# One transpose for both heads' 64 extra keys in the two middle neighbourhood pairs of a one-core encoder kernel

## The chip, the core and the metric

The kernel runs on one core of one Trainium2 chip. The core has five engines that work side by side and wait for one another by semaphores: TensorE (PE in the profile; its weight loads are listed as PEld), VectorE (DVE), ScalarE (ACT), GpSimd (POOL) and SyncE (SP, which here issues most of the DMAs). The metric is the device time of one execution in microseconds (us); lower is better.

## The reference

The network has two layers of width 1024 on 512 tokens. In each layer the normalised input is projected, three branches (differential attention, a convolution module, 2-D neighbourhood attention) work on parts of the projection and are merged by gates; a SwiGLU feed-forward network and a gated embedding follow. The change lies in the neighbourhood attention alone:

```
def neighbourhood_attention(qc, kc, vc, rpb):      # 8 heads of 64, grid of 8 rows x 64 columns
    ...
    s = jnp.einsum('bhwd,bhrwcd->bhwrc', q_r, kn).astype(jnp.float32) * scale
    ...
    a = jax.nn.softmax(s.reshape(B, HC, GRID_W, KR * NA_KC), axis=-1)
    ...
    return jnp.einsum('bhwrc,bhrwcd->bhwd', a, vn)
```

Every query sees all 8 rows and a window of 16 columns. The kernel orders the tokens column by column, so a tile of 128 queries (16 columns) needs a run of 256 neighbouring keys.

## The kernel before

**Precision.** Matrix products are made from fp32 numbers cut in two: a high half, which ScalarE writes by a copy into the type fp32r, and a low half, which VectorE writes by a subtraction (`split`, L156 to L158; its ScalarE part is recorded at L143, its VectorE part at L157). A projection takes three products per block (L177 to L179): high by high, high by low, low by high.

**The order of the work.** TensorE's order is the order in which the Python code emits it. The order on the other engines is made by a scheduler that takes, among the instructions that are ready in its own model of time, the one with the best priority; priority is the order of emission, unless `high_priority(offset=n)` moves an instruction n places forward. Weight blocks (`weights`) are fetched and split with such an offset of up to 400. The 31 taps of the convolution (L160 on VectorE, tile `conv_z`) are emitted a few at a time behind other VectorE work (`background`).

Attention is not written as one stage. It is cut into generators (`natten_unit`, `diff_unit`), whose steps are let in between the chunks of the projections: `tick` counts chunks, `later` queues units with a gap, and each `yield` says how many ticks pass before the unit's next step. So TensorE works on projections while the softmax of a unit runs elsewhere.

**A neighbourhood unit.** The 8 heads form 4 pairs (`pr` 0 to 3), the 512 queries 2 halves. One unit is one head (`u` 0 or 1) of a pair for one half: 16 units for a layer, 32 in all, in the order pair, half, head. In each unit there are two query tiles, and one of the two, the wide one, reaches 64 keys beyond the half's own 256 keys. A unit does this:

- scores of both tiles (L847), a minimum on VectorE (L725), exponentials on ScalarE, and then a ScalarE copy of each tile that scales it by the reciprocal sum (all ScalarE work is recorded at L143; tile `natten_e`);
- three ticks later the transposes of the probabilities: four of 128x128 into the PSUM tile `pt` for the half's own keys (L751), and a fifth into `pt2` for the extra keys (L753 in half 0, L749 in half 1). The fifth transposes 128 keys, of which the unit uses 64;
- the splits of `pt` (into tile `natten_pt`) and of the used half of `pt2` (into tile `natten_a`, named `p2` in the code). `p2` holds the high halves of the 64 keys on one half of the partitions and the low halves on the other;
- two ticks later the products with the values: four of 256 columns (L773) and one of 128 columns for the extra keys (L774; "edge product" below), into the PSUM tile `av`. One `av` of one bank serves both heads of a pair and half, and there is a single buffer of it;
- from `av` the output: a ScalarE copy of 64x256 (high half), a VectorE subtraction (low half) and a VectorE addition, all into tile `natten_y`.

`branch_c` consumes `natten_y` after all pairs, far later. PSUM tiles `pt` and `pt2` share the tag `tr` with two buffers. In pair 0 of layer 0 the splits have a priority of their own (`first`).

Of the kernel before, what the change touches and what calls it, by code (L numbers as in the profile page):

```python
# [20 lines left out]
P = 128  # L21
# [13 lines left out]
NW = 256  # L35
# [26 lines left out]
class Net:  # L62
# [228 lines left out]
    def build(self):  # L291
        nc, tc, a = self.nc, self.tc, self.a
        self.bufs = dict(wr=3, wh=3, wl=3, h=8, qk=2, kh=1, v=4, pt=2, y=5, z=5, x=4, t=7, rp=2,
                         e=2, a=3, r=3, ss=1, sm=8, rc=4, b=2, s=8)
        self.bg, self.w_ahead = BG, 400
        self.pbufs = dict(mm=3, sc=2, tr=2, av=1)
        with tc.tile_pool(name="sb", bufs=1) as self.pool, \
                tc.tile_pool(name="ps", bufs=1, space=PSUM) as self.psum, \
                tc.tile_pool(name="dr", bufs=1, space=DRAM) as dram:
            xs = dram.tile([KD, P, 512], F32, name="xs")  # L300
            self.pis = dram.tile([KD, P, 512], F32, name="pis")
            with tc.manual_schedule(engines={mybir.EngineType.PE}):
                h = self.opening()
                xsrc = a["xT"]
                for i in range(L):
                    h = self.layer(i, h, xsrc, xs)
                    xsrc = xs
# [80 lines left out]
    def small(self):  # L388

        for tag in ("ident", "ones"):  # L390
            self.sb(tag, [P, P], bufs=1)
        for tag in ("onesr", "zeror"):
            self.sb(tag, [P, P], F32R, bufs=1)
        for tag, n in (("b", 2 * NW), ("s", 10), ("sm", 8), ("rc", 4)):
# [9 lines left out]

    def consts(self):
        nc, a = self.nc, self.a
        self.zero_r = self.sb("zeror", [P, P], F32R, bufs=1)
        nc.vector.memset(self.zero_r.bitcast(F32), 0.0)
# [300 lines left out]
    def natten_unit(self, pr, half, u, st4, k2, st, box, y):  # L709

        nc, i = self.nc, self.i
        mm = nc.tensor.matmul
        head = 2 * pr + u
        b = self.sb("b", [P, 2, NW])
        with self.tc.high_priority(offset=100):
            nc.sync.dma_start(b, self.a["bias"][i, head, half])
        es = []
        m = self.sb("s", [P, 6])
        two = self.sb("e", [P, 2, NW + 64])
        for t in range(2):  # L720
# [15 lines left out]
            es.append((e, e[:, own]))  # L736
# [7 lines left out]
        for t, (e, _) in enumerate(es):  # L744
            qt = 2 * half + t
            c0 = 64 * (qt == 2)
            ts = slice(t * P, (t + 1) * P)
            if qt == 2:
                nc.tensor.transpose(pt2, e[:, 0:P], self.ident)  # L749
            for c in range(2):  # L750
                nc.tensor.transpose(pt[:, c, ts], e[:, c0 + c * P:c0 + (c + 1) * P], self.ident)  # L751
            if qt == 1:
                nc.tensor.transpose(pt2, e[:, NW - 64:NW + 64], self.ident)  # L753
            if half != t:
                ws = ts
        pp = self.sb("pt", [P, 2, 2, 256], F32R)
        er, eo = (slice(0, 64), slice(64, P))[::1 if half else -1]
# [10 lines left out]
        av = box[half][:, u]  # L768
        hc = u * 256 + (pr % 2) * P
        cols = slice(hc, hc + P)  # L770
        for n in range(2):
            for k in range(2):
                mm(av, vs[2 * half + n][:, g, cols], pp[:, k, n], start=n == k == 0, stop=False)  # L773
        mm(av[:, ws], vds[g][half][:, cols], p2, start=False, stop=True)  # L774


        qs = slice(half * 256, half * 256 + 256)
        rs, ro = (slice(0, 64), slice(64, P))[::-1 if u else 1]
# [814 lines left out]
```

## Time and profile before

| what | value |
|---|---|
| time, median of 3 runs | 1772.08 us (1771.78 to 1774.45) |
| the profiled execution's own time | 1772.31 us |
| its span, first to last instruction | 1770.5 us |
| TensorE matmul busy | 1764.0 us, 100% of the span |
| TensorE weight loads busy | 1550.4 us, 88% |
| VectorE busy | 1371.0 us, 77% |
| ScalarE busy | 898.3 us, 51% |
| GpSimd busy | 63.5 us, 4% |
| transposes of the neighbourhood units | 160 (128 at L751, 16 at L753, 16 at L749) |
| edge products | 32 (L774) |

The duration of a matmul in the records runs from its start to its modelled end, and matmuls overlap: a 512-column one is listed with about 390 ns, but the next starts about 227 ns after it. What an instruction costs TensorE is read from the distance of starts, not from the duration. The middle pairs' units lie at about 99 to 168 us (layer 0) and 977 to 1047 us (layer 1) of the span.

### The profile page before, as it was taken

To read this page: it belongs to the slowest core of one execution; us is meant where nothing else is said; L and a number is where in the kernel's file an instruction comes from. 1 tells how busy PE (TensorE), PEld (TensorE's weight loads), DVE (VectorE), ACT (ScalarE), POOL (GpSimd) and SP (SyncE) were. 2 spreads that over 40 slices of the span, in tenths; PEclk is the share of its full clock that TensorE was granted. 3 is DMA by queue.
4 is the path that set the end of the run, shared out by engine and by line. 5 is a ranking of instruction groups with operands and counts; after the bars stand their busy time and mean duration, and the time that the engine had idled before them with its cause. 6 is when DMAs were issued, how large, how long until landed. Compare 5 with 4: busy or idle time off the path is not lost.

```text
span 1770.5 us, 26539 instructions
## 1 busy us (share of the span) xinstructions
PE 1764.0 (100%) x10017; PEld 1550.4 (88%) x10017; DVE 1371.0 (77%) x2111; ACT 898.3 (51%) x1482; POOL 63.5 (4%) x102
## 2 busy tenths in 40 slices
PE   9999999999999999999999999999999999999998
PEld 7888888888899899898888888888888998998987
DVE  7689887997877577577796788869878775775776
ACT  5566556325665255255545665563356652542544
POOL 0000000000010000000000000000000100100000
PEclk9999999999999999999999999999999999999999
DMA  5666453335656366253537574423364762763432
GB/s 194 191 191 180 126 140 84 102 99 174 196 156 178 127 167 179 85 143 118 160 122 191 177 183 122 135 84 107 105 197 139 191 191 85 187 173 111 122 111 96
DMA packets 98672, 257.51 MB, mean 145 GB/s; under 512 B 12912, under 2 KB 18160, under 8 KB 98544
## 3 DMA queue, kind: packets, MB, share of 16 engines
q1 hardware_dynamic: 91200, 231.26, 42.0%
q0 software_dynamic: 6336, 23.07, 7.4%
q8 instruction: 79, 1.29, 0.3%
q10 hardware_dynamic: 1008, 1.48, 0.2%
q14 instruction: 49, 0.40, 0.1%
HBM read 216.44 MB, written 7.86 MB: 127 GB/s over the span
## 4 chain that ended last, share of the span: by engine, by line
PE 98%; DMA 1%; DVE 0%; ACT 0%; issue 0%; ACTq 0%
PE ffn_sc L1141 14%; PE ffn_av L1141 7%; PE ffn_mm L178 4%; PE ffn_mm L179 4%; PE ffn_mm L177 4%; PE ffn_tr L1141 4%; PE mergea_mm L179 2%; PE mergea_mm L177 2%; PE mergea_mm L178 2%; PE natten_mm L177 2%; PE diff_sc L847 2%; PE gatec_mm L178 2%; PE natten_mm L178 2%; PE diff_mm L177 2%; PE diff_mm L178 2%; PE natten_mm L179 2%
## 5 line engine op out<-in xcount | busy, mean ns | idle before, releaser
L143 ACT ACTIVATE ffn_wh<-ffn_wr 128x1024 fp32r<-128x1024 f32 (+1 forms) x114 | 116.6, 1028 | 193.3 <-PE ffn_mm L178 102.0
L160 DVE SCALAR_TENSOR_TENSOR conv_z<-glu_z,pre_par,conv_z 128x512 f32<-128x512 f32 x240 | 179.2, 747 | 3.0
L157 DVE TENSOR_TENSOR ffn_wl<-ffn_wr,ffn_wh 128x1024 fp32r<-128x1024 f32 (+1 forms) x114 | 135.1, 1185 | 53.3 <-ACT ffn_wh L143 52.8
L1141 PE MATMUL ffn_sc<-wo_h,ffn_wh 128*128 128x256 f32 x704 | 130.4, 283 | 0.0
L1141 PEld LDWEIGHTS ffn_sc<-wo_h,ffn_wh 128*128 128x128 f32 x704 | 110.4, 192 | 0.8
L1141 PE MATMUL ffn_sc<-wo_h,ffn_wl 128*128 128x256 f32 x352 | 99.6, 283 | 0.0
L177 PE MATMUL ffn_mm<-ffn_z,ffn_wh 128*128 128x512 f32 x240 | 93.4, 389 | 0.0
L178 PE MATMUL ffn_mm<-ffn_z,ffn_wh 128*128 128x512 f32 x240 | 93.4, 389 | 0.0
L179 PE MATMUL ffn_mm<-ffn_z,ffn_wl 128*128 128x512 f32 x240 | 93.4, 389 | 0.0
L157 DVE TENSOR_TENSOR ffn_t<-ffn_mm,wo_r 128x512 f32<-128x512 f32 x48 | 33.1, 690 | 69.2 <-PE ffn_mm L179 69.2
L157 DVE TENSOR_TENSOR ffn_wl<-ffn_rp,ffn_wh 128x1024 fp32r<-128x1024 f32 x44 | 53.8, 1223 | 30.1 <-ACT ffn_wh L143 30.1
L143 ACT ACTIVATE mergea_wh<-mergea_wr 128x1024 fp32r<-128x1024 f32 (+1 forms) x32 | 27.1, 847 | 88.8 <-PE mergea_mm L178 80.4
L1141 PEld LDWEIGHTS ffn_sc<-wo_h,ffn_wl 128*128 128x128 f32 x352 | 67.5, 192 | 0.0
L1141 PE MATMUL ffn_sc<-wo_qk,ffn_wh 128*128 128x256 f32 x352 | 67.1, 283 | 0.0
L1141 PE MATMUL ffn_sc<-wo_v,ffn_wh 128*128 128x256 f32 x352 | 67.1, 283 | 0.0
L1141 PE MATMUL ffn_av<-wo_h,ffn_wh 128*128 128x256 f32 x352 | 65.3, 283 | 0.0
L143 ACT ACTIVATE ffn_wh<-ffn_rp 128x1024 fp32r<-128x1024 f32 x44 | 46.4, 1055 | 29.4 <-PE ffn_mm L178 17.5
L1141 PEld LDWEIGHTS ffn_sc<-wo_qk,ffn_wh 128*128 128x128 f32 x352 | 54.9, 192 | 0.0
L1141 PEld LDWEIGHTS ffn_av<-wo_h,ffn_wh 128*128 128x128 f32 x352 | 54.9, 192 | 0.0
L1141 PEld LDWEIGHTS ffn_sc<-wo_v,ffn_wh 128*128 128x128 f32 x352 | 54.9, 192 | 0.0
L179 PEld LDWEIGHTS ffn_mm<-ffn_z,ffn_wl 128*128 128x128 f32 x240 | 45.1, 188 | 9.4
L946 DVE TENSOR_REDUCE diff_s<-diff_sc 128x1 f32<-128x512 f32 x64 | 42.2, 685 | 14.3 <-PE diff_sc L847 14.3
(737 smaller groups left out, 5632.4 us busy)
## 6 DMA issues: line engine op xcount, KB each, us to landing
ffn_wr<-w_gu SPq DMA_DIRECT2D x66, 512.0 KB, 3.9
ffn_e<-w_gu SPq DMA_DIRECT2D x32, 512.0 KB, 3.4
ffn_e<-w_gu POOLq DMA_DIRECT2D x32, 512.0 KB, 8.1
ffn_wr<-w_fd SPq DMA_DIRECT2D x32, 512.0 KB, 4.3
natten_wr<-w_in SPq DMA_DIRECT2D x16, 512.0 KB, 4.2
natten_b<-bias SPq DMA_DIRECT2D x32, 256.0 KB, 4.0
gatec_wr<-w_in SPq DMA_DIRECT2D x16, 512.0 KB, 4.2
diff_wr<-w_in SPq DMA_DIRECT2D x16, 512.0 KB, 3.9
```

The lines of the kernel that those rows point to most:

```text
L143: i = self.nc.scalar.activation(out, in_, func, **kw)
L157: return self.nc.vector.tensor_tensor(out, a, b, op)
L160: return self.nc.vector.scalar_tensor_tensor(out, a, s, b, op0, op1)
L177: mm(out, wh, ah, start=first, stop=False)
L178: mm(out, wh, al, start=False, stop=False)
L179: mm(out, wl, ah, start=False, stop=last)
L847: self.nc.tensor.matmul(out, st4[:, u, qs], st[:, ks], start=n == 0, stop=n == 1)
L946: nc.vector.tensor_reduce(out=m[:, u:u + 1], in_=sc, op=ALU.max, axis=AX.X, negate=True)
L1141: mm(bank[:, u], w[:, u, kp], t, start=begin and n == 0, stop=False, skip_group_check=True)
```

## The change

In the pairs 1 and 2 (`share`) the two heads of a half share one transpose of the extra keys.

- When a wide tile is scaled, ScalarE no longer scales its 256 own keys by one copy: the 64 extra keys are scaled by one copy into a new tile `edge` (128 queries x 2 heads x 64 keys), the other 192 in place by another.
- The unit of head 0 makes only the four transposes of `pt`, only the four products of L773, and leaves `av` as it is.
- The unit of head 1 makes its four transposes, then one transpose of `edge`, whose result has head 0's 64 keys on the lower partitions and head 1's on the upper. It splits both halves of that, with a priority offset of 100 (`high_priority`), makes its four products, then the edge products of both heads, and then the outputs of both heads.
- Since both heads now accumulate in one bank until the end, only head 0's first product starts the bank anew (`start`).
- `edge` has two buffers. To make room, the constant `zeror` takes one of them at the start, and the filler tile `gap` shrinks from 144 to 16 columns: 256 columns more against 128 and 128 fewer. Later tiles keep their places; `b`, `s`, `sm` and `rc` move by 128 columns.

The pairs 0 and 3 keep their code's work, in a loop over one head.

```
-GAP = 144
+GAP = 16
...
-        for t, (_, own) in enumerate(es):
-            self.act(own, own, AF.Copy, scale=m[:, 4 + t:5 + t])
+        share = pr in (1, 2)
+        if share and u == 0:
+            box["edge", half] = self.sb("edge", [P, 2, 64])
+        near, far = slice(0, NW - 64), slice(NW - 64, NW)
+        if half:
+            near, far = slice(64, NW), slice(0, 64)
+        for t, (_, own, wide) in enumerate(es):
+            scale = m[:, 4 + t:5 + t]
+            if share and wide:
+                self.act(box["edge", half][:, u], own[:, far], AF.Copy, scale=scale)
+                own = own[:, near]
+            self.act(own, own, AF.Copy, scale=scale)
         yield 3
         pt = self.ps("tr", (P, 2, 256))
-        pt2 = self.ps("tr", (P, P))
-        p2 = self.sb("a", [P, P], F32R)
...
+        mine = () if share and u == 0 else (0, 1) if share else (u,)
+        if mine:
+            pt2 = self.ps("tr", (P, P))
+            p2 = self.sb("a", [P, 2, P], F32R)
...
+        if share and u:
+            nc.tensor.transpose(pt2, box["edge", half].rearrange("p a b -> p (a b)"), self.ident)
...
             self.split(pp[:, 0], pp[:, 1], pt)
-            with self.tc.high_priority(offset=100 * (first and half + u == 0)):
-                self.split(p2[er], p2[eo], pt2[er])
+            for v in mine:
+                back = v == 1 if share else half == 0
+                er, eo = (slice(0, 64), slice(64, P))[::-1 if back else 1]
+                with self.tc.high_priority(offset=100 * (share or first and half + u == 0)):
+                    self.split(p2[er, v], p2[eo, v], pt2[er])
...
-                mm(av, vs[2 * half + n][:, g, cols], pp[:, k, n], start=n == k == 0, stop=False)
-        mm(av[:, ws], vds[g][half][:, cols], p2, start=False, stop=True)
+                mm(av[:, u], vs[2 * half + n][:, g, at[u]:at[u] + P], pp[:, k, n],
+                   start=n == k == 0 and not (share and u), stop=False)
+        for v in mine:
+            mm(av[:, v, ws], vds[g][half][:, at[v]:at[v] + P], p2[:, v], start=False,
+               stop=v == u)
...
-        with self.tc.high_priority(offset=100 * (pr == 3)):
-            self.split(y[rs, 0, qs], y[rs, 1, qs], av[rs])
-            self.tt(y[rs, 1, qs], y[rs, 1, qs].bitcast(F32), av[ro], ALU.add)
+        for v in mine:
+            rs, ro = (slice(0, 64), slice(64, P))[::-1 if v else 1]
+            with self.tc.high_priority(offset=100 * (pr == 3)):
+                self.split(y[rs, 0, qs], y[rs, 1, qs], av[rs, v])
+                self.tt(y[rs, 1, qs], y[rs, 1, qs].bitcast(F32), av[ro, v], ALU.add)
```

More of the change, by code (lines that the diff above doesn't have):

```diff
@@ L293, in build @@
         self.bufs = dict(wr=3, wh=3, wl=3, h=8, qk=2, kh=1, v=4, pt=2, y=5, z=5, x=4, t=7, rp=2,
-                         e=2, a=3, r=3, ss=1, sm=8, rc=4, b=2, s=8)
+                         e=2, a=3, r=3, ss=1, sm=8, rc=4, b=2, s=8, edge=2)
         self.bg, self.w_ahead = BG, 400
@@ L391, in small @@
             self.sb(tag, [P, P], bufs=1)
-        for tag in ("onesr", "zeror"):
-            self.sb(tag, [P, P], F32R, bufs=1)
-        for tag, n in (("b", 2 * NW), ("s", 10), ("sm", 8), ("rc", 4)):
+        self.sb("onesr", [P, P], F32R, bufs=1)
+        for tag, n in (("b", 2 * NW), ("s", 10), ("sm", 8), ("rc", 4), ("edge", 2 * 64)):
             self.sb(tag, [P, n])
@@ L406, in consts @@
         nc, a = self.nc, self.a
-        self.zero_r = self.sb("zeror", [P, P], F32R, bufs=1)
+        self.zero_r = self.sb("edge", [P, P], F32R)
         nc.vector.memset(self.zero_r.bitcast(F32), 0.0)
@@ L735, in natten_unit @@
                      accum_out=m[:, 2 + t:3 + t])
-            es.append((e, e[:, own]))
+            es.append((e, e[:, own], wide))
         nc.vector.reciprocal(m[:, 4:6], m[:, 2:4])
-        for t, (_, own) in enumerate(es):
-            self.act(own, own, AF.Copy, scale=m[:, 4 + t:5 + t])
+        share = pr in (1, 2)
[10 more added lines that the diff above has]
+            self.act(own, own, AF.Copy, scale=scale)
         yield 3
         pt = self.ps("tr", (P, 2, 256))
-        pt2 = self.ps("tr", (P, P))
-        p2 = self.sb("a", [P, P], F32R)
-        for t, (e, _) in enumerate(es):
-            qt = 2 * half + t
-            c0 = 64 * (qt == 2)
+        mine = () if share and u == 0 else (0, 1) if share else (u,)
+        if mine:
+            pt2 = self.ps("tr", (P, P))
+            p2 = self.sb("a", [P, 2, P], F32R)
+        for t, (e, _, wide) in enumerate(es):
+            c0 = 64 * (half and wide)
             ts = slice(t * P, (t + 1) * P)
-            if qt == 2:
+            if not share and half and wide:
                 nc.tensor.transpose(pt2, e[:, 0:P], self.ident)
@@ L751, in natten_unit @@
                 nc.tensor.transpose(pt[:, c, ts], e[:, c0 + c * P:c0 + (c + 1) * P], self.ident)
-            if qt == 1:
+            if not share and not half and wide:
                 nc.tensor.transpose(pt2, e[:, NW - 64:NW + 64], self.ident)
-            if half != t:
+            if wide:
                 ws = ts
+        if share and u:
+            nc.tensor.transpose(pt2, box["edge", half].rearrange("p a b -> p (a b)"), self.ident)
         pp = self.sb("pt", [P, 2, 2, 256], F32R)
-        er, eo = (slice(0, 64), slice(64, P))[::1 if half else -1]
         first = pr == self.i == 0
```

6 lines of the change are left out of this document (2 added, 4 removed).

## The prediction, made before the changed kernel was run

> **What bounds the kernel now.** I read the page first: the engines, the granted clock and the chain that ended last. Then I asked for the waits of TensorE, since a kernel whose chain is one engine can gain only from that engine's own instructions or from its waits.
>
> ```profile
> span 1770.5 us, 26539 instructions
> PE 1764.0 (100%) x10017; PEld 1550.4 (88%) x10017; DVE 1371.0 (77%) x2111; ACT 898.3 (51%) x1482; POOL 63.5 (4%) x102
> PEclk9999999999999999999999999999999999999999
> PE 98%; DMA 1%; DVE 0%; ACT 0%; issue 0%; ACTq 0%
> ```
>
> ```profile
> engine line waited for: us in total, times, longest us
> PE pre_av L327 <- DVE pre_zeror L408: 1.1, 1, 1.1
> PE ffn_mm L178 <- DVE ffn_y L157: 0.2, 1, 0.2
> ```
>
> The chain is TensorE, at full clock, and it waits 1.3 us in the whole span: once for the first memset, once in the feed-forward network, never in a neighbourhood unit. So nothing that only makes an operand ready sooner can shorten this kernel. What shortens it is fewer or shorter steps of TensorE; what lengthens it is a new wait of TensorE. The whole question is how many nanoseconds of TensorE the change takes out, and whether some operand becomes late.
>
> A busy matmul isn't a price, as ends overlap. The price is the distance of starts. Three stretches of TensorE's timeline show it around the units of the middle pairs in layer 0:
>
> ```profile
> 108.95 0.60 PE L751 MATMUL natten_tr<-pre_ident,natten_e 128*128 128x128 f32 x4
> 109.38 0.27 PE L753 MATMUL natten_tr<-pre_ident,natten_e 128*128 128x128 f32 x1
> ...
> 115.47 0.64 PE L773 MATMUL natten_av<-natten_pt,natten_v 128*128 128x256 f32 x4
> 115.94 0.23 PE L774 MATMUL natten_av<-natten_a,natten_t 128*128 128x128 f32 x1
> 116.00 0.62 PE L751 MATMUL natten_tr<-pre_ident,natten_e 128*128 128x128 f32 x4
> 116.46 0.27 PE L753 MATMUL natten_tr<-pre_ident,natten_e 128*128 128x128 f32 x1
> 116.49 0.48 PE L177 MATMUL gatec_mm<-glu_h,gatec_wh 128*128 128x512 f32 x1
> 116.81 0.39 PE L178 MATMUL gatec_mm<-glu_h,gatec_wh 128*128 128x512 f32 x1
> ...
> 117.26 0.39 PE L177 MATMUL gatec_mm<-glu_h,gatec_wh 128*128 128x512 f32 x1
> ...
> 122.53 0.64 PE L773 MATMUL natten_av<-natten_pt,natten_v 128*128 128x256 f32 x4
> 123.00 0.23 PE L774 MATMUL natten_av<-natten_a,natten_t 128*128 128x128 f32 x1
> ...
> 129.58 0.64 PE L773 MATMUL natten_av<-natten_pt,natten_v 128*128 128x256 f32 x4
> 130.05 0.23 PE L774 MATMUL natten_av<-natten_a,natten_t 128*128 128x128 f32 x1
> 130.12 0.29 PE L749 MATMUL natten_tr<-pre_ident,natten_e 128*128 128x128 f32 x1
> ```
>
> Four transposes take 109.38 - 108.95 = 0.43 us, 0.1075 each. Two 512-column products take 117.26 - 116.81 = 0.45, 0.225 each. From the edge product at 115.94 to the second projection product at 116.81 there are 0.87 us, which hold one edge product, five transposes (0.54) and one projection product (0.225): the edge product costs about 0.11 us, although the next instruction is recorded 0.06 after it. Units follow one another every 7.05 us (122.53 - 115.47 = 7.06, 129.58 - 122.53 = 7.05).
>
> **The change, part by part.** *Transposes removed.* Two pairs, two halves, two layers are 8 places; in each the unit of head 0 loses its fifth transpose and head 1's remains. 8 x 0.1075 = 0.86 us less, all of it on the path.
>
> "TensorE: Matmul & The Clock Gate" of the Trainium skill, in "Back-to-back issue gap", gives some 81 ns for a 128-column matmul in a stream in which each has a weight load of its own, and 56 ns for an isolated one; by the former it would be an estimate of 8 x 0.081 = 0.65 us. This case's rows show 0.1075, and those count.
>
> *Edge products moved.* Head 0's goes from its own unit to stand right before head 1's. The number of edge products is unchanged. Two of them side by side don't occur in the trace. From below the second costs the distance at which a record follows one, 0.06 (115.94 to 116.00); from above the listed duration of an edge product's weight load:
>
> ```profile
> L774 PEld LDWEIGHTS natten_av<-natten_a,natten_t x32: 188/192/192, 82.0 to 1071.4; 128*128 128x128 f32 x32
> ```
>
> I take 0.11, as now, since the transposes, which like it stream 128 columns behind a load of 128, do stand side by side and need 0.1075: the move costs nothing. The bounds are 8 x (0.06 - 0.11) = -0.4 and 8 x (0.19 - 0.11) = +0.64 us.
>
> *Scaling in two copies.* Each of the 16 wide tiles of these pairs gets one more ScalarE copy. Rows for the size of it:
>
> ```profile
> L143 ACT ACTIVATE natten_a<-natten_tr x32: 257/272/274, 76.1 to 1064.8; 64x128 fp32r<-64x128 f32 x32
> L143 ACT ACTIVATE natten_y<-natten_av x32: 360/378/381, 82.4 to 1071.8; 64x256 fp32r<-64x256 f32 x32
> ...
> 125.12 0.90 ACT L143 ACTIVATE natten_e<-natten_e,natten_s 128x256 f32<-128x256 f32 x2
> 122.00:144.00 22.00, 22.00 (x121) 18.97 (x120) 19.56 (x47) 14.55 (x36) 0.45 (x3) 1.00 0.46 141
> ```
>
> 128 columns more cost 0.106 us (378 - 272), so the part that doesn't depend on columns is 272 - 106 = 166 ns, and that is what a split copy pays twice; 0.27 if overlap is worse. 16 x 0.17 = 2.7 us of ScalarE (at most 4.4). It hides behind ScalarE's idle time, 22.00 - 14.55 = 7.4 us in this stage, and each unit has room: this scaling ends at 126.02 and its transposes start at 130.12, 4.1 us later. Without that room it would be 0.17 per unit on the path, 2.7 in all. I take nothing.
>
> *The low halves put ahead.* VectorE does the same subtractions as before, two for head 1's unit instead of one each. What it stands in now:
>
> ```profile
> 119.58 0.69 DVE L157 TENSOR_TENSOR natten_pt<-natten_tr,natten_pt 128x512 fp32r<-128x512 f32 x1
> 120.19 0.74 DVE L160 SCALAR_TENSOR_TENSOR conv_z<-glu_z,pre_par,conv_z 128x512 f32<-128x512 f32 x1
> 120.85 1.22 DVE L157 TENSOR_TENSOR natten_wl<-natten_wr,natten_wh 128x1024 fp32r<-128x1024 f32 x1
> 122.10 0.29 DVE L157 TENSOR_TENSOR natten_a<-natten_tr,natten_a 64x128 fp32r<-64x128 f32 x1
> ...
> 119.28 1.06 ACT L143 ACTIVATE natten_wh<-natten_wr 128x1024 fp32r<-128x1024 f32 x1 [0.82 <-PE gatec_mm L178]
> ```
>
> The subtraction ends at 122.39 for an edge product at 123.00: 0.61 us to spare, the tightest that I found in the sixteen middle units, because a tap and a weight block stand before it. Ahead of those two, both subtractions would end at about 120.28 + 2 x 0.29 = 120.9, with 2.1 us to spare; if they also go before the 0.69 us one of `pt`, that ends at the same 120.9 for products at 122.53, 1.7 to spare. As no TensorE wait stands here, the earlier end gains nothing. Behind it the tap and the weight block slip by up to 0.58 us. The block has cover: its high half could start when a projection product freed one of three buffers, so two blocks of 24 products, 2 x 24 x 0.225 = 10.8 us, lie before its use. Were that cover gone, 8 x 0.58 = 4.6 us.
>
> *Output of head 0 delayed.* This is the new wait. Before, head 0's sums left `av` while TensorE went on for 7 us; now both heads' products end together and all six evacuating instructions come after. Behind them on TensorE stands the next half's first product, which needs the single `av` buffer back, and behind that every projection. From the end of the last edge product, 123.00 + 0.23 = 123.23, to 129.58 there are 6.35 us. The evacuation of one head in that place:
>
> ```profile
> 124.76 0.43 DVE L157 TENSOR_TENSOR natten_y<-natten_av,natten_y 64x256 fp32r<-64x256 f32 x1
> 125.25 0.69 DVE L157 TENSOR_TENSOR natten_pt<-natten_tr,natten_pt 128x512 fp32r<-128x512 f32 x1
> 125.98 0.42 DVE L157 TENSOR_TENSOR natten_y<-natten_y,natten_av 64x256 fp32r<-64x256 f32 x1
> ```
>
> It ends at 126.40, 3.17 us after the products, again the slowest that I found in the middle pairs. The second head adds at least one copy and two VectorE instructions, 0.38 + 0.43 + 0.42 = 1.23 if none overlaps: 4.40, 1.95 to spare. With a tap (0.74) before each of the two it is 5.88, 0.47 to spare. I take no wait. Other queues are passed by nothing: no DMA moves, the memsets on POOL stay, and the changed places of small tiles cost nothing that a row here would show.
>
> *Sum.* -0.86 + 0 + 0 + 0 = -0.86 us, bounds -1.26 to -0.22 before any stall. The profiled execution would go from 1772.31 (1770.5 of span and 1.8 around it) to 1771.45. The median of the runs is 0.23 lower, 1772.08, so 1771.2.
>
> **The rivals.** *Slower: `av` comes back late.* The mechanism is the one above, decided at 6.35 us from the last edge product to the last read. VectorE has 19.56 us of work in the 22.00 us of that stage, so every further instruction can find a queue. If each of head 1's two VectorE instructions finds a weight block (1.22) before it, and one of them a tap too, the evacuation takes 4.40 + 2.44 + 0.74 = 7.58 us, 1.23 late. At the four places of layer 0 that is 4.9 us, and -0.86 + 4.9 = +4.1: 1776.2. Against it: it needs the worst neighbour twice at every place, and one head at its slowest has 3.2 us in hand today. For it: `natten_y` has no priority in the middle pairs.
>
> "PSUM — Partial Sum Buffer" of the Trainium skill, under "PSUM bank collisions raise a hardware error", says that two engines must not touch the same bank and quadrant at one time, reads included; that would make the two heads' evacuation one chain, as I took it. No row here shows two engines reading `av` at once or not.
>
> *Eaten up: a few short waits.* If two of the eight places find a weight block before both instructions (4.40 + 2.44 = 6.84, 0.49 late), 1.0 us returns: 1772.2. With 0.3 us late at all eight it is 1772.08 - 0.86 + 2.4 = 1773.6.
>
> *Faster by more than 0.2%.* It would need 3.5 us. All waits of TensorE are 1.3 us and the removed work 0.86; not even 2.2 together. Only a reordering elsewhere that shortens TensorE's steps could do it, and no row points to one.
>
> *It doesn't do what it says.* A weight block is itself emitted with a priority of up to 400 places, so 100 may not carry the subtractions past it. Then the second one ends at about 122.39 + 0.29 = 122.68, still 0.3 before 123.00: the same 1771.2. A further block (1.22) before it would be 0.9 late, at one place: 1772.1.
>
> **How the numbers follow.** A measurement of this kernel can tell about 0.2% (3.5 us) from no change. The forecast case, -0.86 without a wait, with or without the low halves moved ahead: 0.70. Short waits that eat it up: 0.21. `av` late by over a microsecond in layer 0: 0.07. Faster by over 3.5 us: 0.02. The first two are within 0.2%: 0.91. The range takes the lower bound of the sum and nearly the 0.3 us by which the lowest run lies under the median (1772.08 - 1.26 - 0.3 = 1770.5) and goes up to the eaten-up case, 1773.6; outside lie the last two and a bit of the second.
>
> **What would show it.** Right: the transposes of the units fall from 160 to 152, TensorE's waits stay at those two rows, the middle units have four transposes in head 0 and two edge products about 0.06 to 0.19 apart in head 1, and the last VectorE read of `av` ends before the next half's L773. Wrong in size: the two edge products cost other than 0.11. Wrong in kind: a wait of L773 for VectorE's `natten_y` (the slow rival), of the edge product for `natten_a` (priority without effect), or new waits far from the units, which would mean that the scheduler's order changed elsewhere; any TensorE wait of over 1 us that is not in the list above refutes the forecast.

## The result and the profile after

The changed kernel takes 1775.94 us (median of 18 runs, 1774.06 to 1778.66) against 1772.44 for the kernel before on the same chips: a ratio of 1.0019, 95% interval 1.0012 to 1.0026. One of the 18 runs of the kernel before took 1924.79 us where the others took 1771.78 to 1774.45, and the ratio is of the others. By the bound of the prediction (0.2%) that is no change, but the interval lies above 1, and the time lies outside the range, 2.3 us over its upper end. The profiled execution took 1777.07 us, with a span of 1775.3 us; it is 1.1 us above its median, and 4.76 above the profiled execution of the kernel before (1772.31), where the medians differ by 3.5.

From the page of the kernel after, the span, the engines and the chain:

```profile
span 1775.3 us, 26542 instructions
...
PE 1765.6 (99%) x10009; PEld 1551.0 (87%) x10009; DVE 1372.5 (77%) x2111; ACT 902.3 (51%) x1498; POOL 63.5 (4%) x102
...
PE 98%; DVE 1%; DMA 0%; ACT 0%; issue 0%; SPq 0%; ACTq 0%; DVEq 0%
```

Eight matmuls fewer, and yet a longer span. VectorE appears on the chain with 1%. The waits of TensorE in the kernel after name the place:

```profile
engine line waited for: us in total, times, longest us
PE natten_av L789 <- DVE natten_a L157: 2.8, 2, 1.6
PE pre_av L327 <- DVE pre_edge L407: 1.1, 1, 1.1
PE diff_mm L177 <- ACT gatec_x L143: 0.6, 1, 0.6
```

An edge product (now L789) waits for the low halves `natten_a`. TensorE's timeline of the kernel after shows the wait of layer 0, and it isn't in a changed unit. It is in the second unit of pair 3 (start, duration, engine, operation; idle time and its releaser in brackets):

```profile
179.75 0.63 PE L786 MATMUL natten_av<-natten_pt,natten_v 128*128 128x256 f32 x4
181.59 0.30 PE L789 MATMUL natten_av<-natten_a,natten_t 128*128 128x128 f32 x1 [1.21 <-DVE natten_a L157]
```

The same edge product in TensorE's timeline of the kernel before:

```profile
179.43 0.23 PE L774 MATMUL natten_av<-natten_a,natten_t 128*128 128x128 f32 x1
```

VectorE's timeline ahead of it, first in the kernel before, then in the kernel after:

```profile
175.53 0.69 DVE L157 TENSOR_TENSOR natten_pt<-natten_tr,natten_pt 128x512 fp32r<-128x512 f32 x1
176.25 0.29 DVE L157 TENSOR_TENSOR natten_a<-natten_tr,natten_a 64x128 fp32r<-64x128 f32 x1
...
177.27 1.22 DVE L157 TENSOR_TENSOR diff_wl<-diff_wr,diff_wh 128x1024 fp32r<-128x1024 f32 x1
```

```profile
178.63 0.69 DVE L157 TENSOR_TENSOR natten_pt<-natten_tr,natten_pt 128x512 fp32r<-128x512 f32 x1
179.24 0.74 DVE L160 SCALAR_TENSOR_TENSOR conv_z<-glu_z,pre_par,conv_z 128x512 f32<-128x512 f32 x1
179.90 1.22 DVE L157 TENSOR_TENSOR diff_wl<-diff_wr,diff_wh 128x1024 fp32r<-128x1024 f32 x1
181.15 0.29 DVE L157 TENSOR_TENSOR natten_a<-natten_tr,natten_a 64x128 fp32r<-64x128 f32 x1
```

Before, the low halves followed `pt` at once and were 2.9 us early (176.54 against 179.43). After, a tap and a weight block stand between, `pt` itself is 3.1 us later, and the low halves end at 181.44, 0.15 before the edge product starts: it starts on their release. "PSUM — Partial Sum Buffer" of the Trainium skill says under "Engine vs sequencer instructions" that VectorE's queue is a strict first in, first out; the trace agrees, the 0.29 us subtraction starts when the block before it is done.

**Where the time came in.** I aligned TensorE's instructions of both profiled executions, one of each kernel, and took the shift of each (its start after, less its start before, both from the start of the span). The shift grows by 0.89 us up to 100 us, by -0.10 and -0.16 over the middle pairs of the two layers, by 1.49 and 3.03 over pair 3 of the two layers, by 0.23 around 250 us, and by -0.63 at 587 us, where the kernel before loses something in its feed-forward network that none of the other traces has. It ends at 4.76. What lies outside the pairs comes and goes between kernels whose code is the same there (at 60 us the shift is between -0.04 and 0.70 in the runs below; at 82 us an edge product of pair 0 waits for a DMA in some profiles and not in others, 1.05 us in experiment 7 and 1.30 in 9), so I count the middle pairs (the change's own work) and pair 3 (the loss). "Growth" below is the growth of the shift over a stretch, layer 0 and layer 1.

In layer 1 the 3.03 has three parts: 0.3 at the first unit's edge product, 0.9 at a projection that waits for a buffer behind ScalarE's late work (the third row of the waits, 0.6 of it), and 1.8 at the second unit's edge product.

### The profile page after: what moved, and what is told of

Its sections match the earlier page's. It is cut to its first block, busy times and chain, and to the rows that moved or that the text cites. A ratio compares the mean times of both kernels' runs of the same rounds, so it can differ in the third digit from the quotient of the medians.

```text
span 1775.3 us, 26542 instructions
## 1 busy us (share of the span) xinstructions
PE 1765.6 (99%) x10009; PEld 1551.0 (87%) x10009; DVE 1372.5 (77%) x2111; ACT 902.3 (51%) x1498; POOL 63.5 (4%) x102
## 4 chain that ended last, share of the span: by engine, by line
PE 98%; DVE 1%; DMA 0%; ACT 0%; issue 0%; SPq 0%; ACTq 0%; DVEq 0%
PE ffn_sc L1158 14%; PE ffn_av L1158 7%; PE ffn_mm L178 5%; PE ffn_mm L177 4%; PE ffn_mm L179 4%; PE ffn_tr L1158 4%; PE mergea_mm L179 2%; PE mergea_mm L177 2%; PE mergea_mm L178 2%; PE natten_mm L177 2%; PE diff_sc L864 2%; PE natten_mm L178 2%; PE natten_mm L179 2%; PE gateb_mm L178 2%; PE gateb_mm L179 2%; PE gateb_mm L177 2%
## 5 line engine op out<-in xcount | busy, mean ns | idle before, releaser
L177 PEld LDWEIGHTS ffn_mm<-ffn_z,ffn_wh 128*128 128x128 f32 x240 | 45.1, 188 | 9.3
```

Of the source, the lines that this page charges most:

```text
L177: mm(out, wh, ah, start=first, stop=False)
```

## Experiments

Each kernel was timed against the kernel before on the same chip (before: 1772.73 us for numbers 1 to 4, 1772.55 for 5 to 8, 1772.62 for 9 to 12). The theory at the start was that the two heads' outputs, now late and one after the other, push VectorE's work back into pair 3; a second suspect stood on SP's queue. The rows of SP, in the kernel before and after (SPq rows are issues of DMAs):

```profile
161.99 1.24 SPq L866 DMA_DIRECT2D diff_rp<-diff_rp  x2
164.00 0.33 SPq L171 DMA_DIRECT2D diff_wr<-w_va  x1
```

```profile
159.32 0.51 SPq L883 DMA_DIRECT2D diff_rp<-diff_rp  x1
...
164.68 0.33 SPq L171 DMA_DIRECT2D diff_wr<-w_va  x1
165.06 0.54 SPq L883 DMA_DIRECT2D diff_rp<-diff_rp  x1
```

The last rotation copy of the differential attention stood ahead of a weight load before, and stands behind it after. The load waits for a buffer (VectorE's block at 163.43 is done at 164.65, the load goes out at 164.68), the copy waits with it, and VectorE, in order, waits for the copy (in the kernel before not at all in layer 0, 0.40 us in layer 1). VectorE's timeline of the kernel after:

```profile
169.50 0.69 DVE L157 TENSOR_TENSOR diff_rp<-diff_rp,diff_r 128x512 f32<-128x512 f32 x1 [0.66 <-DMA diff_rp<-diff_rp]
...
1050.08 0.69 DVE L157 TENSOR_TENSOR diff_rp<-diff_rp,diff_r 128x512 f32<-128x512 f32 x1 [2.23 <-DMA diff_rp<-diff_rp]
```

The results together. "Waits" says at which units of pair 3 the edge product started within 0.15 us of the low halves' end, that is, on their release (first unit, second unit):

| kernel | median us | ratio and interval | growth, middle pairs | growth, pair 3 | waits, layer 0; layer 1 |
|---|---|---|---|---|---|
| after | 1775.94 | 1.0019 [1.0012, 1.0026] | -0.10, -0.16 | 1.49, 3.03 | second; both |
| 1 no priority | 1775.79 | 1.0017 [1.0008, 1.0026] | -0.10, -0.16 | 1.97, 2.08 | second; second |
| 2 priority alone | 1772.81 | 1.0000 [0.9992, 1.0009] | 0, 0 | 0, 0 | none |
| 3 two copies alone | 1772.81 | 1.0001 [0.9992, 1.0009] | 0, 0 | 0, 0 | none |
| 4 late outputs alone | 1774.12 | 1.0008 [0.9999, 1.0017] | 0, 0 | 0.39, 0.43 | first; first |
| 5 rotation first | 1774.00 | 1.0007 [0.9999, 1.0016] | -0.11, -0.16 | 0.39, 1.39 | first; first |
| 6 rotation behind | 1773.30 | 1.0006 [0.9997, 1.0015] | 0, 0 | 0, 0 | none |
| 7 priority in pair 3 | 1773.27 | 1.0003 [0.9994, 1.0011] | -0.09, -0.16 | 0, 0 | none |
| 8 pair 2 alone | 1777.00 | 1.0024 [1.0014, 1.0033] | 1.39, -0.07 | 0.87, 1.45 | second; second |
| 9 edge products apart | 1773.20 | 1.0001 [0.9992, 1.0010] | -0.11, -0.19 | 0, 0 | none |
| 10 late outputs and rotation behind | 1773.84 | 1.0004 [0.9995, 1.0013] | 0, 0 | 0, 0.31 | none |
| 11 pair 1 alone | 1773.02 | 1.0000 [0.9991, 1.0008] | 0.13, -0.09 | 0, 0 | none |
| 12 outputs with priority | 1775.88 | 1.0018 [1.0009, 1.0027] | -0.09, -0.16 | 1.91, 1.59 | second; second |

**1, no priority.** The kernel after without the new priority.

```
-                with self.tc.high_priority(offset=100 * (share or first and half + u == 0)):
+                with self.tc.high_priority(offset=100 * (first and half + u == 0)):
```

> The changed kernel without the priority of the middle pairs' low halves; all else stays. In the changed kernel's trace TensorE waits at pair 3: the edge product waits for VectorE's natten_a at 181.59 us (1.4 us later against its neighbours), 1052.42 and 1062.18 (1.8 us), and the shift against before grows there by 1.5 us in layer 0 and 3.0 us in layer 1. Theory A, the outputs: both heads' outputs of a half now come out of one bank as one chain (copy, subtraction, addition, then the same again: the second copy starts 0.04 us after the first addition ends), and after pair 2 this chain pushes the score minima, exponentials and splits of pair 3 back. Then taking the priority away changes nothing in kind: pair 3 still waits, the ratio to before stays near 1.002 (1775 to 1777 us), natten_a of pair 3 late again. Theory B, the priority: the taps and weight blocks that the low halves overtake pile up ahead of pair 3. Then the waits in pair 3 go and the time falls to about 1772 us, or new waits appear in the middle pairs instead.

The loss stays: 1775.79 us, pair 3 grows by 1.97 and 2.08. The priority of the middle pairs' low halves is not its cause.

**2, priority alone.** The kernel before, with the priority in the middle pairs.

```
-            with self.tc.high_priority(offset=100 * (first and half + u == 0)):
+            with self.tc.high_priority(offset=100 * (pr in (1, 2) or first and half + u == 0)):
```

> The kernel before with one edit: the low halves of pairs 1 and 2 get the priority of 100 places; every head keeps its own transpose, edge product and output. Theory A (outputs in one chain): ratio 1.000 within 0.0006, no wait of TensorE in pair 3. Theory B (overtaken taps and weights pile up): waits of the edge products of pair 3 for natten_a of 3 us or more in all, ratio near 1.002.

1772.81 us, no wait in pair 3, no growth: nothing lost and nothing gained.

**3, two copies alone.** The kernel before, with the scaling of the wide tiles of the middle pairs in two copies.

```
+            if pr in (1, 2) and half != t:
+                self.act(own[:, far], own[:, far], AF.Copy, scale=scale)
+                own = own[:, near]
             self.act(own, own, AF.Copy, scale=scale)
```

> The kernel before with one edit: in the pairs 1 and 2 ScalarE scales each wide tile by two copies in place (192 and 64 columns), 16 copies more. Theories A and B: ratio 1.000 within 0.0006, no wait of TensorE in pair 3. Theory C, ScalarE: the added copies put off the exponentials and splits behind them, so that pair 3's natten_a comes late; then waits there and a ratio near 1.002. ScalarE busy should rise by 16 times 0.17 to 0.27 us, 2.7 to 4.4 us, in all cases.

1772.81 us, no growth. ScalarE's busy time rises from 898.3 to 902.4 us and nothing waits for it.

**4, late outputs alone.** The kernel before, with the outputs of both heads after head 1's products in the middle pairs; transposes and edge products as they were.

```
-        with self.tc.high_priority(offset=100 * (pr == 3)):
+        for v in () if late and u == 0 else (0, 1) if late else (u,):
+            av = box[half][:, v]
+            rs, ro = (slice(0, 64), slice(64, P))[::-1 if v else 1]
...
```

> The kernel before with one edit: in the pairs 1 and 2 both heads' outputs are taken from the sums after head 1's products, as the change does; transposes, edge products, scaling and priorities are those of before. Theory A: this alone brings the waits of TensorE at pair 3's edge products for natten_a and a ratio near 1.002 (between 1.001 and 1.003). Theories B and C: ratio 1.000 within 0.0006 and no such waits. If the next half's first product waits for natten_y instead, the sums' single buffer is the limit, which is the slow rival of the prediction.

1774.12 us. Pair 3 grows by 0.39 and 0.43, in both layers at its first unit, whose edge product starts at 173.41. VectorE's timeline of this kernel:

```profile
170.61 0.42 DVE L157 TENSOR_TENSOR natten_y<-natten_y,natten_av 64x256 fp32r<-64x256 f32 x1
171.05 1.23 DVE L157 TENSOR_TENSOR diff_wl<-diff_wr,diff_wh 128x1024 fp32r<-128x1024 f32 x1
172.20 0.74 DVE L160 SCALAR_TENSOR_TENSOR conv_z<-glu_z,pre_par,conv_z 128x512 f32<-128x512 f32 x1
172.97 0.29 DVE L157 TENSOR_TENSOR natten_a<-natten_tr,natten_a 64x128 fp32r<-64x128 f32 x1
```

The second head's addition, a weight block and a tap stand before the low halves, which began at 168.95 in the kernel before. So the late outputs alone do a part of it, 0.8 of 4.5 us.

**5, rotation first.** The kernel after, with the third load of w_va ordered behind the last rotation copy, as in the kernel before (`behind` adds an order without a wait of its own).

```
+            if self.phase == 'diff' and o == 2:
+                self.behind(self.load, self.rot)
```

> The changed kernel with one edit to SyncE's queue: the third block of the value weights of the differential attention (w_va) is issued after the last rotation copy of that branch's first head, as in the kernel before. In the changed kernel that copy stands behind the block's load, which waits for its buffer; the copy is issued at 165.06 us, lands late, and VectorE stands still 0.66 us in layer 0 and 2.23 us in layer 1 before the rotation product, with the second head's last addition and pair 3's score minima behind it in order. Theory S, SyncE's queue: this is most of the loss. Then the growth of the shift in pair 3 falls from 1.5 and 3.0 us to about what the late outputs alone gave, 0.4 and 0.4 us, and the ratio from 1.0019 to 1.0000 to 1.0006 (1772.5 to 1773.8 us). Theory A, the outputs in one chain, without the queue: nothing changes, ratio 1.0015 to 1.002, waits of 1.4 us and more for natten_a in pair 3.

1774.00 us; pair 3 grows by 0.39 and 1.39, 1.78 in all instead of 4.5, now at its first unit: as the theory has it in layer 0, and 1 us more in layer 1. So the order on SP had a part in the loss.

**6, rotation behind.** The kernel before with the opposite order, `self.behind(self.rot, self.load)`.

> The converse: the kernel before with one edit, the last rotation copy of the first differential head is issued behind the third block of w_va, as in the changed kernel. Theory S: VectorE waits for that copy (more than 0.5 us at the rotation product of that head), the score minima of pair 3 come late, and TensorE waits at pair 3, 0.5 to 3 us in all; ratio 1.0003 to 1.0017. Theory A: no wait of TensorE in pair 3, ratio 1.0000 within 0.0005. If VectorE waits but TensorE doesn't, the queue harms only together with the late outputs.

1773.30 us, no wait of TensorE in pair 3, no growth. VectorE does wait for the copy, 1.28 us in layer 0 and 1.30 in layer 1, but the low halves of pair 3 still end 1.67 us or more before their products. Alone, the order on SP costs nothing.

**7, priority in pair 3.** The kernel after, with the priority of the low halves extended to the last pair.

```
-                with self.tc.high_priority(offset=100 * (share or first and half + u == 0)):
+                with self.tc.high_priority(offset=100 * (pr > 0 or first and half + u == 0)):
```

> The changed kernel with the priority of 100 places for the low halves of pair 3 as well. Theories S and A say alike that what TensorE waits for in pair 3 is natten_a, which stands behind a tap and a weight block. With the priority these two are overtaken (1.96 us sooner) and the waits for natten_a go; the products of pair 3's four own blocks, which had 0.42 and 0.04 us to spare, become the next limit, so at most 0.3 us of growth in each layer is left: ratio 0.9998 to 1.0005. If the time stays at 1.0015 or more, the wait is set further back than at that place in VectorE's order (by ScalarE's late copies of the transposes), and the priority has nothing to move.

1773.27 us, growth 0 and 0. The place that lost 1.21 us, in VectorE's and in TensorE's timeline of this kernel:

```profile
177.74 0.29 DVE L157 TENSOR_TENSOR natten_a<-natten_tr,natten_a 64x128 fp32r<-64x128 f32 x1
178.06 0.75 DVE L160 SCALAR_TENSOR_TENSOR conv_z<-glu_z,pre_par,conv_z 128x512 f32<-128x512 f32 x1
178.87 0.69 DVE L157 TENSOR_TENSOR natten_pt<-natten_tr,natten_pt 128x512 fp32r<-128x512 f32 x1
179.47 0.74 DVE L160 SCALAR_TENSOR_TENSOR conv_z<-glu_z,pre_par,conv_z 128x512 f32<-128x512 f32 x1
180.13 1.22 DVE L157 TENSOR_TENSOR diff_wl<-diff_wr,diff_wh 128x1024 fp32r<-128x1024 f32 x1
```

```profile
180.76 0.64 PE L786 MATMUL natten_av<-natten_pt,natten_v 128*128 128x256 f32 x4
181.23 0.23 PE L789 MATMUL natten_av<-natten_a,natten_t 128*128 128x128 f32 x1
```

SP's order is that of after. In layer 0 the last output addition of pair 2 ends 4.70 us behind the start of the last edge product (4.58 after), and `pt` ends 1.20 us before its products (0.42 after, 2.73 before). The low halves go ahead of tap and block, and end 3.2 us before their product instead of on it. In layer 1 more has changed than their place: that addition ends after 4.63 us instead of 6.16, and VectorE waits 0.33 us for the copy instead of 2.23.

The whole growth in pair 3 is gone. But 0.27 and 0.17 us come in right behind it, which the kernel after doesn't have: the first product of the differential attention takes over the bank of `av`, and it starts 0.15 us after the last addition of pair 3 (198.62 + 0.42 = 199.04; after, that addition is 1.53 us early). So 4.1 of the 4.5 us are gained. VectorE's and TensorE's timelines:

```profile
198.62 0.42 DVE L157 TENSOR_TENSOR natten_y<-natten_y,natten_av 64x256 fp32r<-64x256 f32 x1
```

```profile
199.19 0.47 PE L623 MATMUL diff_av<-diff_wh,glu_h 128*128 128x512 f32 x1
```

**8, pair 2 alone.** The kernel after with `share = pr == 2`.

> The changed kernel with the shared transpose in pair 2 alone; pair 1 stays as before. It keeps the same order in SyncE's queue (last rotation copy behind the w_va block) and the chain of both heads' outputs right ahead of pair 3. Theories S and A: waits for natten_a in pair 3 as in the changed kernel, 1 to 4 us in all, ratio 1.001 to 1.0025. A theory in which the loss piles up over both middle pairs: half of it, ratio 1.0005 to 1.001. TensorE's own gain in the shared places should be half that of the changed kernel, where the shift fell by 0.033 us at each of 8 places, 0.26 in all.

1777.00 us. The loss in pair 3 is there (0.87 and 1.45), and in layer 0 a wait that the kernel after doesn't have: `av` comes back 1.20 us late in pair 2. TensorE's timeline:

```profile
159.14 0.71 PE L786 MATMUL natten_av<-natten_pt,natten_v 128*128 128x256 f32 x4 [1.20 <-DVE natten_y L157]
```

That is the slow rival of the prediction, at one place of the four.

**9, edge products apart.** The kernel of experiment 7, with head 0's edge product ahead of head 1's four products.

```
+        if share and u:
+            mm(av[:, 0, ws], vds[g][half][:, at[0]:at[0] + P], p2[:, 0], start=False, stop=False)
         for n in range(2):
             for k in range(2):
...
-        for v in mine:
+        for v in mine[-1:]:
```

> The kernel after with the last pair's low halves moved ahead too (as in the run with the priority for the last pair) and, besides, head 0's edge product put ahead of head 1's four products, so that the two edge products no longer stand next to each other. Mis-sized term theory: a second 128-column product right behind the first costs about 0.15 us where a lone one behind the four 256-column products costs 0.08, so the change saves only 0.03 us a place; apart, the growth over the two middle pairs falls from -0.10 and -0.16 us a layer to about -0.4 us a layer (four places, 0.11 of a transpose each), no wait for natten_a stays, and the end lies 0.5 to 0.6 us below that of the run with the priority alone, if the start is equal. Rival (an edge product costs the same wherever it stands): the growth stays at -0.10 and -0.16. The time cannot tell them apart: 1772 to 1773.3 us by both.

1773.20 us; the middle pairs grow by -0.11 and -0.19 instead of -0.09 and -0.16. The rival holds: an edge product costs as much apart as side by side. (Behind pair 3, 0.12 and 0.14 us come in as in experiment 7.) TensorE's timeline of this kernel:

```profile
124.59 0.22 PE L785 MATMUL natten_av<-natten_a,natten_t 128*128 128x128 f32 x1
124.65 0.69 PE L788 MATMUL natten_av<-natten_pt,natten_v 128*128 128x256 f32 x4
125.18 0.23 PE L791 MATMUL natten_av<-natten_a,natten_t 128*128 128x128 f32 x1
125.24 0.61 PE L761 MATMUL natten_tr<-pre_ident,natten_e 128*128 128x128 f32 x4
```

The next product starts 0.06 us after the lone edge product, but the four behind it then take 0.53 instead of 0.47: what isn't paid at its own place is paid by the next.

**10, late outputs and rotation behind.** Experiments 4 and 6 in one kernel.

> The kernel before, transposes and scaling as they were, with two things of the kernel after put in: both heads' outputs after head 1, and the last rotation copy behind the third load of w_va on SP's queue. Alone they cost 0.4 + 0.4 us and nothing. Theory that the two together make the loss: the copy holds VectorE right ahead of the last pair, on top of the late additions; TensorE waits for natten_a in both layers, growth in the last pair over 1 us a layer, as after (1.5 and 3.0), time 1775 to 1776 us. Rival (they add up, and the rest of the loss came with the priority or the shared transposes): growth 0.4 a layer as with late outputs alone, 1773.5 to 1774.2 us.

1773.84 us, growth 0 and 0.31: the time is the rival's, and the growth is even less than in experiment 4 alone. The 0.31 comes in at a projection, as a part of the loss after did, and another 0.40 behind pair 3, where the last addition is late for the differential attention as in experiment 7. The theory that the two together make the loss falls. VectorE's timeline shows why the edge products don't wait:

```profile
168.41 0.29 DVE L157 TENSOR_TENSOR natten_a<-natten_tr,natten_a 64x128 fp32r<-64x128 f32 x1
168.73 0.42 DVE L157 TENSOR_TENSOR natten_y<-natten_y,natten_av 64x256 fp32r<-64x256 f32 x1
169.39 0.69 DVE L157 TENSOR_TENSOR diff_rp<-diff_rp,diff_r 128x512 f32<-128x512 f32 x1 [0.25 <-DMA diff_rp<-diff_rp]
```

In this kernel the scheduler's order has the low halves ahead of the instruction that waits for the copy, more than 4 us earlier than in experiment 4 (172.97).

**11, pair 1 alone.** The kernel after with `share = pr == 1`.

> The kernel after with the change in the second of the four pairs alone; the third is as before. Theory that the loss arises where the late outputs of the third pair meet the last pair's work on VectorE, and not in the shared units themselves: no wait for natten_a, growth in the last pair below 0.1 us in both layers, growth over the two middle pairs about -0.05 to -0.1 us, and time 1772 to 1773 us, no difference that can be measured. Rival (each shared pair costs its part wherever it stands): about half of the loss, 1774 us, with waits in the unit after the second pair.

1773.02 us, no wait in pair 3. The middle pairs of layer 0 lose 0.13, where a gain of 0.05 to 0.1 was expected (0.18 comes in at the first unit of pair 2); those of layer 1 gain 0.09. The list of waits names nothing there, but it is the same mechanism, one pair earlier: pair 2 isn't shared in this kernel, its low halves have no priority, in VectorE's timeline they stand behind a weight block, and in TensorE's the edge product starts 0.15 us after their end (144.26):

```profile
142.71 1.23 DVE L157 TENSOR_TENSOR gatec_wl<-gatec_wr,gatec_wh 128x1024 fp32r<-128x1024 f32 x1
143.97 0.29 DVE L157 TENSOR_TENSOR natten_a<-natten_tr,natten_a 64x128 fp32r<-64x128 f32 x1
```

```profile
144.41 0.30 PE L789 MATMUL natten_av<-natten_a,natten_t 128*128 128x128 f32 x1
```

So a shared pair that isn't followed by pair 3 costs next to nothing here, but not because the wait is absent.

**12, outputs with priority.** The kernel after, with priority for the output copies and additions of the middle pairs.

```
-            with self.tc.high_priority(offset=100 * (pr == 3)):
+            with self.tc.high_priority(offset=100 * (share or pr == 3)):
```

> The kernel after with priority for the additions and copies of both heads' outputs in the middle pairs; SP's order keeps the last rotation copy behind the load. Theory that late rotation alone costs nothing and the outputs' lateness is the half that makes it dear: outputs move ahead of the taps, but they already follow one another in a chain, so part stays: growth in the last pair 0.5 to 1.5 us over both layers against 4.5 after, time 1773 to 1774.5 us. Rival (the copy behind the load is the whole cost): the growth stays near 4.5 and the time at 1775.5 us or more.

1775.88 us, growth 1.91 and 1.59: over the forecast of 0.5 to 1.5 and under the rival's 4.5, with the rival's time. The second unit's low halves again stand behind a tap and a block and end at 181.46 for a product at 181.61. The priority brings the last addition of pair 2 forward in layer 1 (it ends 4.72 us behind the start of the edge product, 6.16 after), where the growth falls, and not in layer 0 (5.03, 4.58 after), where it rises. So this kernel doesn't tell what outputs that are earlier in both layers would do.

**What they say together.** In every kernel with a growth of 0.39 or more in pair 3, low halves of that pair ended within 0.15 us of their product; where none did, the growth is 0, once 0.31. Experiment 7 changes the priority of just these copies, and the growth there goes, in layer 0 with late outputs and SP's order still in place. So the loss is the place of the unprioritised low halves of pair 3 in VectorE's order: directly where an edge product starts on their release, 3.6 of the 4.5 us; for the 0.9 at the projection in layer 1 it is only shown that it goes with them. The moved places of the small tiles are not it: the kernels of 7, 9 and 11 have them too, and no growth in pair 3. Late outputs and the order on SP matter only through the order that the scheduler then makes: together they cost less in pair 3 (10) than the outputs alone (4), and the load order helps (5) or does nothing (6). Why the scheduler puts the low halves of pair 3 behind tap and block in one kernel and not in the next I can't tell from these runs; that its order changed is shown, what tipped it stays open. The reverse, pushing only these copies back in the kernel before, wasn't tried.

No version beats the kernel before by more than its measurement can tell: the lowest ratio is 1.0000 (2 and 11), and 9, which shares both pairs, is at 1.0001.

## Why the prediction was wrong, point by point

- **Bound.** Right, TensorE's chain; what lengthens the kernel is a new wait of TensorE, and it did.
- **Transposes removed.** Right in number: 152, 128 at L761 and 8 each at L759, L763 and L767.
- **Edge products moved, taken at 0.** The mis-sized term. TensorE's timeline in the kernel after:

```profile
116.27 0.64 PE L786 MATMUL natten_av<-natten_pt,natten_v 128*128 128x256 f32 x4
116.74 0.60 PE L761 MATMUL natten_tr<-pre_ident,natten_e 128*128 128x128 f32 x4
117.17 0.27 PE L767 MATMUL natten_tr<-pre_ident,natten_edge 128*128 128x128 f32 x1
117.20 0.48 PE L177 MATMUL gatec_mm<-glu_h,gatec_wh 128*128 128x512 f32 x1
...
123.28 0.64 PE L786 MATMUL natten_av<-natten_pt,natten_v 128*128 128x256 f32 x4
123.75 0.34 PE L789 MATMUL natten_av<-natten_a,natten_t 128*128 128x128 f32 x2
123.93 0.62 PE L761 MATMUL natten_tr<-pre_ident,natten_e 128*128 128x128 f32 x4
124.31 0.47 PE L177 MATMUL gatec_mm<-glu_h,gatec_wh 128*128 128x512 f32 x1
```

  Head 0's stretch takes 117.20 - 116.27 = 0.93 us without its edge product; it took 116.49 - 115.47 = 1.02 before. Head 1's takes 124.31 - 123.28 = 1.03 us with two edge products and four transposes. By the shifts a steady place of the middle pairs gains 0.073 in head 0's stretch and loses 0.040 in head 1's. The prediction's 0.1075 for a transpose holds: at the first place of each layer, where only a transpose goes, the shift falls by 0.107 and 0.105. So the added edge product costs 0.15 where the removed one had cost 0.07 (at the last place of each layer, where only an edge product is added, the shift grows by 0.12). All 8 places save 0.10 + 0.16 = 0.26 us instead of 0.86. The term was +0.6, near its upper bound of +0.64. Its cause isn't that the two stand side by side (experiment 9).
- **Scaling in two copies.** Right: ScalarE's busy time rose by 4.0 us (forecast 2.7, at most 4.4), hidden. The group of the new copies in the kernel after gives their price, 340 ns each for 64 columns:

```profile
L143 ACT ACTIVATE natten_edge<-natten_e,natten_s 128x64 f32<-128x64 f32 x16 | 5.4, 340 | 3.9 <-DVE natten_s L736 3.9
```

- **Low halves put ahead.** Right: nothing gained (experiments 1 and 2).
- **Output of head 0 delayed, no wait taken.** Right for `av` in the kernel after, though barely: at the tightest place the last addition ended 0.20 us before the products that need the bank, where 1.95 to spare were forecast and 0.47 with two taps. In experiment 8 it was 1.20 late. The outputs of the two heads were one chain, as assumed; in VectorE's and ScalarE's timelines of the kernel after, for instance, the second head's copy starts 0.04 us after the first head's last addition (167.23 + 0.42 = 167.65):

```profile
167.23 0.42 DVE L157 TENSOR_TENSOR natten_y<-natten_y,natten_av 64x256 fp32r<-64x256 f32 x1
```

```profile
167.69 0.38 ACT L143 ACTIVATE natten_y<-natten_av 64x256 fp32r<-64x256 f32 x1
```

  By the rule of "PSUM — Partial Sum Buffer" in the Trainium skill, under "PSUM bank collisions raise a hardware error", the two engines must not be in one bank and quadrant together; the trace agrees, their accesses don't overlap.
- **"Other queues are passed by nothing: no DMA moves".** The step that failed: in the sum, the stall that was taken at 0. I looked for what the change itself moves, and behind the delayed outputs at `av` alone, and took the order of everything else on SP and VectorE as fixed. Both orders are made anew by the scheduler. A rotation copy fell behind a load, VectorE's order ahead of pair 3 changed, and the unprioritised low halves there came behind a tap and a block: +4.5 us in the profiled execution and 3.5 in the medians, against a range that held 1.5 above the kernel before. The prediction looked for a late `natten_a` only in the middle pairs, where it had the priority, and named new waits elsewhere only as a sign of error, without a chance and a price. In the kernel before these same copies of pair 3 were 2.5 to 4.7 us early; at the second unit, one tap and one block (0.74 + 1.22 us) and a `pt` that came 3.1 us later used up its 2.9.

## What to carry to other kernels

Where a scheduler orders the engines, an edit in one stage is an edit of the order in the next: before predicting, list the operands behind the edited stage that have no priority, how early each is, and what could stand before it. Give the short copy that TensorE waits for its own priority in every stage, not just in the stage that is edited: here that took the 4.5 us out of pair 3 in the trace, of which 0.4 came back behind it. And price an instruction by taking it out and putting it in, since the same 128-column product was worth 0.07 us at one place and 0.15 at another.

## What the runs showed that I had not expected

A delayed input can take a wait away: the rotation copy put behind the load, on top of late outputs, lowered the growth in pair 3 from 0.39 and 0.43 to 0 and 0.31, by way of the scheduler's order. In layer 1, 0.40 came in behind pair 3 instead, and the times (ratios of 1.0004 and 1.0008, with intervals that overlap) can't be told apart. And kernels whose code is alike up to 60 us of the span differ there by up to 0.74 us (shifts of -0.04 to 0.70), as much as the change could have saved.
